# Banded heads of a hybrid decoder layer: turns and value products moved later in the round, weights split sooner, query chunks laid out evenly

## The chip, the cores and the metric

The kernel runs on one core of one Trainium2 chip. The metric is the device time of one execution in microseconds, the median of the runs shown. The profile is one execution taken by the hardware profiler; its times count from the first instruction. TensorE is called PE in its rows, VectorE DVE, ScalarE ACT, GpSimd POOL, and SyncE, which here only sends transfers, SP.

## What is computed

One decoder layer on 2048 tokens of width 1024. The input is RMS-normalised and modulated, projected once, and feeds two kinds of heads side by side: eight heads of causal attention with a cumulative forget gate (called fox below), and eight banded heads, which look back over 128 keys, with rotary positions and one learned sink per head. Both outputs are gated, concatenated, projected, normalised and added to the input. The part that the change touches is the banded one:

```python
def sliding_window_sink_attention(q, k, v, sinks):
    qb = q.reshape(B, nb, Q_BLOCK, SWA_KV_HEADS, SWA_GROUP, d)
    kk, vv = with_prev(k), with_prev(v)
    s = jnp.einsum('bnqhgd,bnshd->bnhgqs', qb, kk, preferred_element_type=jnp.float32) * (d ** -0.5)
    rel = i + Q_BLOCK - j
    band = (rel >= 0) & (rel < WINDOW)
    s = jnp.where(mask[None, :, None, None], s, -jnp.inf)
    p = jax.nn.softmax(jnp.concatenate([s, sink], axis=-1), axis=-1)[..., :-1]
    out = jnp.einsum('bnhgqs,bnshd->bnqhgd', p.astype(vv.dtype), vv)

def reference(x, c, positions, w_ada, b_ada, g_pre, w_in, b_fgate, sinks, w_out, g_post):
    ...
        h = rms_norm(x, g_pre[l]) * (1.0 + scale[:, None, :]) + shift[:, None, :]
        qa, ka, va, fa, za, qb, kb, vb, zb = jnp.split(h @ w_in[l], split_points, axis=-1)
        oa = forgetting_attention(...) * jax.nn.silu(za)
        ob = sliding_window_sink_attention(rope(qb), rope(kb), vb, sinks[l]) * jax.nn.silu(zb)
        y = jnp.concatenate([oa, ob], axis=-1) @ w_out[l]
        x = x + gate[:, None, :] * rms_norm(y, g_post[l])
```

## The kernel before

Every matmul operand is held as two float16 halves, a high one and what is left of it, and each product is made of three matmuls (high by high, high by low, low by high). The order on all engines is written out by hand: what the Python code issues first stands first in its engine's queue, and engines meet through semaphores.

**Stages.** The input is normalised and turned (up to some 130 us, with the keys and values of the banded heads); then comes the banded stage (some 155 to 430 us), in which projections of gates (`zb`), fox values (`va`) and banded queries (`qb`) are the filling between the steps of the banded heads; then the fox stage with its own projections (`qk`, `za`), and last the output projection.

**Units.** A projection of one weight column block (a key such as `zb2`, 128 columns) and one chunk of 512 tokens is cut into eight units of three matmuls of 512 columns (`proj_units`, L335) or twelve of 128 (`value_units`, L351). The list `punits` holds them all; `fill(n)` (L1092) issues the next n. `events` hangs the preparation of a key's weights on unit numbers ahead of its first unit: `w_load` (a transfer of 512 KB by GpSimd's queue), `w_max` (the largest magnitude on VectorE, sent out to memory), `w_back` (read back for all partitions), `w_scale`, `w_high` (ScalarE), `w_low` twice (VectorE), `w_done`. The table in `add` (L944) gives each step its lead in units; `zb0` and `zb1` have leads of their own. The raw weights share two buffers, the halves of `zb` and `va` two more, those of `qb` one.

**Ticks.** `after(n, f)` puts f off by n ticks; `tick()` runs what is due. So a chunk's evacuation is spread behind its last unit: a gate takes a tanh and a product one and two ticks later, a query chunk (`evac_rope`, L725) a copy and a half swap through SP one tick later, then cosine at 2, sine at 7, and the halves at 8 and 9. The swap's buffers `qf` and `qs` are single.

**The banded heads** work in 32 pairs (`Pair`, L859; four pairs of heads by eight pairs of query blocks), one round each. The steps of a pair: `scores` (12 matmuls into the one bank pair `pss`), `maxima` (VectorE: a predicated copy folds the two key blocks into one, then the maximum), `exps` (four exponentials on ScalarE into `sm_`), `turn` (four transposes into `pxb`), `split` one tick later (ScalarE copies the high half to `fold`, VectorE subtracts the low one, GpSimd masks each twice into `ptt`, whose rows the profile calls ptb), `pv` (24 matmuls) and an output step one tick later (VectorE, then a store by GpSimd's queue). A query chunk serves two pairs.

A round (L1128 to L1155) issues 8 or 9 units in four parts with a tick ahead of each. Maxima follow the first tick, exponentials the second, and the end of the round is, on TensorE, `pv` of the pair before, `turn` of this pair and `scores` of the next. The list of units in this stage (L1018 to L1036) alternates query chunks with others by the numbers `lim`; several others remain for the end.

Of the kernel before, what the change touches and what calls it, by code (L numbers as in the profile page):

```python
# [11 lines left out]
F16 = mybir.dt.float16  # L12
# [4 lines left out]
ALU = mybir.AluOpType  # L17
AX = mybir.AxisListType

P = 128  # L20
# [4 lines left out]
CH = 512  # L25
# [18 lines left out]
def hybrid_layer(  # L44
# [17 lines left out]
    V, A, G, PE, SP = nc.vector, nc.scalar, nc.gpsimd, nc.tensor, nc.sync  # L62
# [20 lines left out]
    def sm(n, tag):  # L83
        return small.tile([P, n], F32, tag=tag, name=tag)
# [117 lines left out]
    def after(n, f):  # L202
        late.append([n, f])

    def tick():
        now = [f for n, f in late if n <= 1]
        late[:] = [[n - 1, f] for n, f in late if n > 1]
        for f in now:
            f()
# [15 lines left out]
    def w_max(key):  # L225
        mx = sm(1, "w_mx")
        V.tensor_reduce(mx[:], wq[key][0][:], axis=AX.XY, op=ALU.max, apply_absolute_value=True)
        md = mx_d[len(kaps_seen) % 3]
        kaps_seen.append(key)
        G.dma_start(md[:], mx[:])  # L230
        wq[key].append(md)
# [224 lines left out]
    st = start.enter_context(tc.tile_pool(name="start", bufs=1, reuse_waits="tile"))  # L456
    wad = start.enter_context(tc.tile_pool(name="wad", bufs=8, reuse_waits="tile"))
    with tc.manual_schedule():
# [95 lines left out]
        for _ in range(3):  # L554
            e = math.floor(math.log2(rest))
# [154 lines left out]
    def swa_pool(name, bufs, **kw):  # L710
        return swa.enter_context(tc.tile_pool(name=name, bufs=bufs, reuse_waits="tile", **kw))
# [3 lines left out]
    stp = swa_pool("stp", 2)  # L715
# [143 lines left out]
    class Pair:  # L859
# [40 lines left out]
        def turn(self):  # L900

            px = ps_t.tile([P, 4, P], F32, tag="t", name="pxb")
            for n in range(4):
                PE.transpose(px[:, n, :], self.sm_[:, n, 1:P + 1], ident[:])
            self.ptt = ptp.tile([P, 2, 2, 4, P], F16, tag="pt", name="ptb")
            fold = ptp.tile([P, 2, 4, P], F16, tag="fo", name="fold")

            def split():
                A.activation(fold[:, 0], px[:], AF.Copy)
                V.tensor_tensor(fold[:, 1], px[:], fold[:, 0], op=ALU.subtract)  # L910
                self.rinv = sm(4, "b_ri")
                V.reciprocal(self.rinv[:], self.rs[:])
                for n in range(2):
                    G.affine_select(self.ptt[:, 0, n], fold[:, n], [[0, 4], [-1, P]], ALU.is_ge, 0.0,
                                    base=-1, channel_multiplier=1)
                    G.affine_select(self.ptt[:, 1, n], fold[:, n], [[0, 4], [1, P]], ALU.is_ge, 0.0,
                                    base=0, channel_multiplier=-1)

            after(1, split)

        def pv(self):
            j, i = self.j, self.i
            po = ps_pv.tile([P, 4, 64], F32, tag="pv", name="pob")
            for e, (i_, k0, nk) in enumerate(self.blocks):
                for h in range(2):
                    for b in range(nk):
                        for n, (pp_, vv) in enumerate(((0, 0), (0, 1), (1, 0))):
                            PE.matmul(po[:, 2 * e + h, :], self.ptt[:, b + 2 - nk, pp_, 2 * e + h, :],  # L928
                                      vb[:, k0 + b, self.g, 64 * vv:64 * vv + 64],
                                      start=(b == 0 and n == 0), stop=(b == nk - 1 and n == 2))  # L930

            def out_():
                on = onp.tile([P, 2, P], F32, tag="on", name="on")
                V.tensor_tensor(on[:].rearrange("p e (h d) -> p (e h) d", h=2), po[:],
                                self.rinv[:].unsqueeze(2).broadcast_to([P, 4, 64]), op=ALU.mult)
                o_store(on[:], onp, i // 4, slice((i % 4) * P, (i % 4 + 2) * P), slice((4 + j) * P, (5 + j) * P), G, 1)

            after(1, out_)
# [5 lines left out]
    def add(key, us):  # L944
        if key not in pkeys and key not in ("kb", "vb"):
            at = len(punits) - {"za3": 4}.get(key, 20 if key[:2] == "za" else 0)
            for n, (lead, f) in enumerate(((42, lambda: w_load(key, pieces(key))), (31, lambda: w_max(key)),
                                           (21, lambda: w_back(key)), (12, lambda: w_scale(key)),
                                           (9, lambda: w_high(key)), (7, lambda: w_low(key, 0)),
                                           (5, lambda: w_low(key, 1)), (4, lambda: w_done(key)))):  # L950
                if n >= 4 and key[:2] in ("qk", "za"):
                    lead -= 1
                if n < 4 and key == "qb0":
                    lead += (16, 14, 12, 4)[n]
                if key == "zb1":
                    lead = at - (6, 38, 46, 67, 71, 73, 75, 77)[n]
                if key == "zb0":
                    if n >= 3:
                        events.setdefault((13, 13, 14, 15, 16)[n - 3], []).append(f)
                else:  # L960
                    events.setdefault(max(at - lead, n), []).append(f)
        if key not in pkeys:
            pkeys.append(key)
        punits.extend(us)

    events = {}
    others = []
    for kind, j in (("zb", 0), ("zb", 1), ("va", 0), ("zb", 2), ("zb", 3), ("va", 1), ("va", 2)):
        key = f"{kind}{j}"
# [55 lines left out]
    qbs = [(f"qb{c_ // 4}", qb_units(c_ // 4, c_ % 4)) for c_ in range(2, 16)]  # L1025
    n_o = 7
    for n, (key, us) in enumerate(qbs):
        add(key, us)
        lim = (7, 8, 8)[n] if n < 3 else 5 + 5 * (n + 1) // 4 if n + 1 < len(qbs) else len(others)
        for key2, us2 in others[n_o:lim]:  # L1030
            add(key2, us2)
        n_o = lim
# [56 lines left out]
    windows = [Pair(j, i) for j in range(4) for i in range(0, NB, 2)]  # L1089
    pos = [0]  # L1090

    def fill(n, each=None):  # L1092

        for _ in range(n):
            for f in events.pop(pos[0], []):
                f()
            punits[pos[0]]()
            pos[0] += 1
            if each:
                each()  # L1100
# [9 lines left out]
    with swa_order:  # L1110
        fill(N_PRO - 4, tick2)
        psx.close()
        sws = swa_pool("sws", 1)
        ptp = swa_pool("ptp", 1)
        ps_s = swa_pool("ps_s", 1, space=PSUM)
        ps_t = swa_pool("ps_t", 1, space=PSUM)
        ps_pv = swa_pool("ps_pv", 1, space=PSUM)
        wsp = swa_pool("wsp", 2)
        wss, wst = sm(16, "a_m"), sm(2, "wst")
        wsq = {}  # L1120
        base = N_PRO
        NW = len(windows)
        windows[0].scores()
        windows[0].maxima()
        fill(2, tick2)
        windows[0].exps()
        fill(2, tick2)
        for n, wd in enumerate(windows):  # L1128
            goal = base + (N_SWA - base) * (n + 1) // NW
            todo = goal - pos[0]  # L1130
            part = [todo * (m + 1) // 4 - todo * m // 4 for m in range(4)]
            tick()
            if n:
                wd.maxima()
            fill(part[0])
            tick()
            if n:
                wd.exps()
            fill(part[1])
            tick()  # L1140
            fill(part[2])
            tick()
            fill(part[3])
            if n:
                windows[n - 1].pv()
            wd.turn()
            if n + 1 < NW:
                windows[n + 1].scores()

            if n:  # L1150
                A.activation(wsq[n - 1][:], wsq[n - 1][:], AF.Square, accum_out=wss[:, (n - 1) % 16:(n - 1) % 16 + 1])
            if n == 16:
                V.tensor_reduce(wst[:, 0:1], wss[:], axis=AX.X, op=ALU.add)
            wsq[n] = wsp.tile([P, 2 * P], F32, tag="wsq", name="wsq")
            SP.dma_start(wsq[n][:], w_out0[n // 4 * P:(n // 4 + 1) * P, n % 4 * 2 * P:(n % 4 + 1) * 2 * P])  # L1155
        tick()
        fill(5)
        tick()
        fill(5)
        tick()  # L1160
        fill(6)
        windows[NW - 1].pv()
        tick()
        tick()
        A.activation(wsq[NW - 1][:], wsq[NW - 1][:], AF.Square, accum_out=wss[:, 15:16])
        V.tensor_reduce(wst[:, 1:2], wss[:], axis=AX.X, op=ALU.add)
        wsum = sm(1, "w_mx2")
        V.tensor_reduce(wsum[:], wst[:], axis=AX.X, op=ALU.add)
# [16 lines left out]
    stp = foxl.enter_context(tc.tile_pool(name="stpa", bufs=3, reuse_waits="tile"))  # L1185
# [404 lines left out]
    with tc.manual_schedule():  # L1590
# [34 lines left out]
        for s, stp_ in enumerate(steps):  # L1625
# [11 lines left out]
            a = b = 0  # L1637
# [100 lines left out]
```

## Time and profile before

| | us |
|---|---|
| median of 3 runs | 1173.02 (1172.4 to 1174.38) |
| the profiled execution | 1175.42 |
| its span, first to last instruction | 1173.7 |
| TensorE busy over the span | 1129.2 |
| TensorE busy, 480 to 940 us (fox) | 454.18 of 460 |
| TensorE busy, 1000 to 1174 us (output) | 165.17 of 174 |
| mean granted clock of TensorE | 0.991 of full |

A row of a group gives line, engine, operation and tiles, how often, and times; "idle before" is the time its engine stood, with what ended it. A row of the timeline gives start, duration, engine, line and tiles, and in brackets the idle time just before it with its releaser; neighbours of one kind are merged. In the table by stretches each engine has its busy time and its number of instructions, and PEclk is the share of full clock that TensorE was granted. A busy TensorE may still contain short waits between merged matmuls.

### The profile page before, as it was taken

To read this page: it belongs to the slowest core of one execution; us is meant where nothing else is said; L and a number is where in the kernel's file an instruction comes from. 1 tells how busy PE (TensorE), PEld (TensorE's weight loads), DVE (VectorE), ACT (ScalarE), POOL (GpSimd) and SP (SyncE) were. 2 spreads that over 40 slices of the span, in tenths; PEclk is the share of its full clock that TensorE was granted. 3 is DMA by queue.
4 is the path that set the end of the run, shared out by engine and by line. 5 is a ranking of instruction groups with operands and counts; after the bars stand their busy time and mean duration, and the time that the engine had idled before them with its cause. 6 is when DMAs were issued, how large, how long until landed. Compare 5 with 4: busy or idle time off the path is not lost.

```text
span 1173.7 us, 26784 instructions
## 1 busy us (share of the span) xinstructions
PE 1129.2 (96%) x10637; PEld 671.6 (57%) x10637; DVE 920.0 (78%) x2137; ACT 661.1 (56%) x1150; POOL 196.6 (17%) x332
## 2 busy tenths in 40 slices
PE   6899999999999999999999999999999999999997
PEld 2476545765558976555555565555556555544444
DVE  7777448687776748788888989887897897778885
ACT  2775325455554521476766667676666788543332
POOL 1122124446445521010000100001000000000000
PEclk9899999999999999999999999999999999999999
DMA  9933342424243333423435331222311237677743
GB/s 334 314 101 88 92 70 53 98 53 118 79 73 90 72 69 64 67 61 81 73 71 77 96 60 51 61 53 65 51 34 46 69 86 230 135 216 200 195 144 108
DMA packets 123482, 120.19 MB, mean 102 GB/s; under 512 B 64948, under 2 KB 100828, under 8 KB 123356
## 3 DMA queue, kind: packets, MB, share of 16 engines
q1 hardware_dynamic: 112088, 85.69, 27.0%
q0 software_dynamic: 10832, 32.50, 13.7%
q8 instruction: 83, 1.36, 0.6%
q14 instruction: 43, 0.35, 0.2%
q10 hardware_dynamic: 436, 0.28, 0.1%
HBM read 64.75 MB, written 25.18 MB: 77 GB/s over the span
## 4 chain that ended last, share of the span: by engine, by line
PE 73%; DVE 13%; DMA 6%; ACT 3%; issue 2%; SPq 1%; POOL 1%; ACTq 0%; DVEq 0%
PE bk L344 27%; PE bk L1531 13%; PE bk L362 5%; PE sta L1320 4%; PE sta L1319 4%; PE bk L1270 4%; PE poa L1345 3%; PE poa L1346 3%; PE poa L1343 3%; DMA wa<-in_w_ada_dram 2%; DVE a_m L1273 2%; DVE pha L1333 1%; PE pob L928 1%; PE pss L875 1%; PE bk L781 1%
## 5 line engine op out<-in xcount | busy, mean ns | idle before, releaser
L1326 ACT ACTIVATE p<-sta,lift,scl_qk 128x1024 f32<-128x1024 f32 (+2 forms) x160 | 171.8, 1074 | 130.9 <-PE sta L1320 81.9
L344 PE MATMUL bk<-hT,wh_qk 128*128 128x512 f16 x768 | 194.7, 378 | 0.0
L1333 DVE TENSOR_TENSOR pha<-p,pha 128x1024 f16<-128x1024 f32 (+2 forms) x160 | 169.1, 1057 | 0.2 <-ACT pha L1330 0.2
L1273 DVE TENSOR_REDUCE a_m<-bk 128x1 f32<-128x512 f32 x192 | 130.4, 686 | 48.8 <-PE bk L1270 47.9
L1531 PE MATMUL bk<-wohl,oz 128*128 128x512 f16 x744 | 165.3, 379 | 1.0 <-DVE oz L1480 0.7
L1330 ACT ACTIVATE pha<-p 128x1024 f16<-128x1024 f32 (+2 forms) x160 | 148.1, 926 | 6.0 <-PE poa L1346 1.2
L1531 PEld LDWEIGHTS <-oz 128*128 128x128 f16 x744 | 71.8, 99 | 82.8 <-DVE oz L1480 1.8
L1346 PE MATMUL poa<-vt,pha 128*128 128x65 f16 x1088 | 116.1, 192 | 1.4 <-DVE pha L1333 1.4
L1343 PE MATMUL poa<-vt,pha 128*128 128x65 f16 x1088 | 116.6, 193 | 0.8 <-DVE ona L1352 0.7
L1345 PE MATMUL poa<-vt,pha 128*128 128x64 f16 x1088 | 116.6, 194 | 0.0
L344 PEld LDWEIGHTS <-wh_qk 128*128 128x128 f16 x768 | 72.2, 97 | 74.4 <-issue 1.9
L1270 PE MATMUL bk<-T 66*128 66x512 f16 (+2 forms) x320 | 109.7, 348 | 5.2 <-DVE a_m L1273 1.9
L1319 PE MATMUL sta<-T 128*128 128x512 f16 (+1 forms) x320 | 110.9, 346 | 2.8 <-ACT p L1326 2.7
L1343 PEld LDWEIGHTS <-pha 128*128 128x128 f16 x1088 | 101.5, 96 | 15.5 <-DVE ona L1352 1.9
L1320 PE MATMUL sta<-T 69*128 69x512 f16 (+1 forms) x320 | 109.8, 348 | 0.0
L1345 PEld LDWEIGHTS <-pha 128*128 128x128 f16 x1088 | 100.9, 97 | 11.4
L1346 PEld LDWEIGHTS <-pha 128*128 128x128 f16 x1088 | 100.8, 99 | 1.8 <-DVE pha L1333 1.8
L344 PE MATMUL bk<-hT,wh_za 128*128 128x512 f16 x384 | 99.7, 378 | 0.0
L362 PE MATMUL bk<-wh_va,hT 128*128 128x128 f16 x1536 | 90.6, 219 | 2.5 <-DVE wh_va L267 2.5
L362 PEld LDWEIGHTS <-hT 128*128 128x128 f16 x1536 | 87.3, 98 | 7.3 <-issue 5.1
L344 PE MATMUL bk<-hT,wh_zb 128*128 128x512 f16 x384 | 90.1, 382 | 0.0
L344 PE MATMUL bk<-hT,wh_qb 128*128 128x512 f16 x384 | 87.3, 379 | 0.0
(457 smaller groups left out, 1906.0 us busy)
## 6 DMA issues: line engine op xcount, KB each, us to landing
hT<-in_x_dram SPq DMA_DIRECT2D x20, 512.0 KB
wa<-in_w_ada_dram SPq DMA_DIRECT2D x16, 512.0 KB
z_d<-tz POOLq DMA_DIRECT2D x32, 256.0 KB, 2.9
T<-stq SPq DMA_DIRECT2D x64, 128.0 KB
T<-z_d SPq DMA_DIRECT2D x16, 512.0 KB
out_dram<-hT SPq DMA_DIRECT2D x15, 512.0 KB
xt<-in_x_dram SPq DMA_DIRECT2D x12, 512.0 KB
qs<-qf SPq DMA_DIRECT2D x80, 64.0 KB
```

Source lines behind the costliest of these rows:

```text
L344: PE.matmul(ps, whl[:, a, k, :], hT[ci][:, b, k, :], start=(k == 0 and n == 0), stop=(k == KT - 1 and n == 2))
L362: PE.matmul(ps[:, u * P:(u + 1) * P], hT[ci][:, a, k, u * P:(u + 1) * P], whl[:, b, k, :], start=(k == 0 and n == 0), stop=(k == KT - 1 an ...
L1270: PE.matmul(mx[:, :w], T[0:XM, 0, i * P:(i + 1) * P], T[0:XM, 2, pc * CH:pc * CH + w], start=True, stop=True)
L1273: V.tensor_reduce(m3[:, u, pc:pc + 1], mx[:, :w], axis=AX.X, op=ALU.max)
L1319: PE.matmul(self.st[:, o:o + w], T[:, 3, kb_], T[:, 1, qc], start=True, stop=False)
L1320: PE.matmul(self.st[:, o:o + w], T[0:XR, 2, kb_], T[0:XR, 0, qc], start=False, stop=not diag)
L1326: A.activation(self.p32[:, :self.w], self.st[:, :self.w], AF.Exp, scale=scl[f"qk{self.hd}"][:], bias=lift[:])
L1333: V.tensor_tensor(self.ph[:, 1, :self.w], self.p32[:, :self.w], self.ph[:, 0, :self.w], op=ALU.subtract)
L1343: PE.matmul(po[:, u, :], ph[:, 0, pq], vt[:, b, hd, 0:65], start=(self.first and n == 0 and u == 0), stop=False)
L1345: PE.matmul(po[:, u, 0:64], ph[:, 0, pq], vt[:, b, hd, 65:VW], start=False, stop=False)
L1346: PE.matmul(po[:, u, :], ph[:, 1, pq], vt[:, b, hd, 0:65], start=False, stop=(self.last and n == len(self.blocks) - 1))
L1531: PE.matmul(py, self.hl[:, i, k, :], w_slot(8 * j + k)[:, cc], start=(k == 0 and m_ == 0), stop=(k == KT - 1 and m_ == 2))
```

## The change

Four things. The masked halves of a pair go to two tiles of their own, from one pool for even pairs and from another (the pool `stp`, whose two buffers nothing else uses in this stage) for odd ones, so two pairs can be under way; the exponentials get a second buffer. In the round, `turn` of pair n-1 follows the second part and `pv` of pair n-2 the third, where before `turn` of pair n and `pv` of pair n-1 stood at its end; behind the last round two turns and products are left instead of one product. The leads of `zb` and `va` keys grow by 8 units, that of `va1` by 18 (`zb0` and `zb1` keep theirs, which are set below). And `lim` lets one other chunk follow each query chunk, sometimes two.

```diff
-            self.ptt = ptp.tile([P, 2, 2, 4, P], F16, tag="pt", name="ptb")
+            even = (8 * self.j + self.i // 2) % 2 == 0
+            self.ptt = [ptp.tile([P, 2, 4, P], F16, tag=f"pt{b}", name="ptb") if even else
+                        stp.tile([P, 2, CH], F16, tag="st", name="ptb") for b in range(2)]
+            ptt = [t[:].rearrange("p a (n c) -> p a n c", n=4) if not even else t[:] for t in self.ptt]
+            self.ptt = ptt
             fold = ptp.tile([P, 2, 4, P], F16, tag="fo", name="fold")
...
                 for n in range(2):
-                    G.affine_select(self.ptt[:, 0, n], fold[:, n], [[0, 4], [-1, P]], ALU.is_ge, 0.0,
+                    G.affine_select(ptt[0][:, n], fold[:, n], [[0, 4], [-1, P]], ALU.is_ge, 0.0,
                                     base=-1, channel_multiplier=1)
-                    G.affine_select(self.ptt[:, 1, n], fold[:, n], [[0, 4], [1, P]], ALU.is_ge, 0.0,
+                    G.affine_select(ptt[1][:, n], fold[:, n], [[0, 4], [1, P]], ALU.is_ge, 0.0,
                                     base=0, channel_multiplier=-1)
...
-                            PE.matmul(po[:, 2 * e + h, :], self.ptt[:, b + 2 - nk, pp_, 2 * e + h, :],
+                            PE.matmul(po[:, 2 * e + h, :], self.ptt[b + 2 - nk][:, pp_, 2 * e + h, :],
...
                 if n < 4 and key == "qb0":
                     lead += (16, 14, 12, 4)[n]
+                if key[:2] in ("zb", "va"):
+                    lead += 18 if key == "va1" else 8
                 if key == "zb1":
                     lead = at - (6, 38, 46, 67, 71, 73, 75, 77)[n]
...
-        lim = (7, 8, 8)[n] if n < 3 else 5 + 5 * (n + 1) // 4 if n + 1 < len(qbs) else len(others)
+        lim = 7 + 6 * (n + 1) // 5 if n + 1 < len(qbs) else len(others)
...
-        sws = swa_pool("sws", 1)
+        sws = swa_pool("sws", 2)
...
             fill(part[1])
+            if n:
+                windows[n - 1].turn()
             tick()
             fill(part[2])
+            if n > 1:
+                windows[n - 2].pv()
             tick()
             fill(part[3])
-            if n:
-                windows[n - 1].pv()
-            wd.turn()
             if n + 1 < NW:
                 windows[n + 1].scores()
...
         tick()
         fill(5)
+        windows[NW - 1].turn()
         tick()
         fill(5)
+        windows[NW - 2].pv()
         tick()
         fill(6)
         windows[NW - 1].pv()
```

## The prediction, before the change was run

> **What bounds the kernel now.** I read the page first, then the busy times by stretch for the stage the change touches (about 155 to 430 us), then the waits of TensorE there, then its instructions in order of time.
>
> ```profile
> span 1173.7 us, 26784 instructions
> PE 1129.2 (96%) x10637; PEld 671.6 (57%) x10637; DVE 920.0 (78%) x2137; ACT 661.1 (56%) x1150; POOL 196.6 (17%) x332
> PE 73%; DVE 13%; DMA 6%; ACT 3%; issue 2%; SPq 1%; POOL 1%; ACTq 0%; DVEq 0%
> ```
>
> TensorE is busy 96% of the span and is 73% of the chain that ended last. The change adds and removes no matmul, so it can only take away stretches in which TensorE stands still or runs slowly. How many are there in the banded stage?
>
> ```profile
> core 0: us, PE busy (x) PEld busy (x) DVE busy (x) ACT busy (x) POOL busy (x), PEclk, DMA share, GB/s
> 155.00:210.00 55.00, 50.76 (x486) 30.35 (x484) 37.30 (x93) 24.36 (x76) 18.66 (x31) 0.97 0.40 70
> 210.00:260.00 50.00, 49.55 (x600) 33.86 (x597) 37.77 (x89) 26.51 (x85) 22.83 (x35) 1.00 0.31 72
> 260.00:310.00 50.00, 50.00 (x412) 26.63 (x411) 38.71 (x93) 26.10 (x84) 25.84 (x41) 1.00 0.36 93
> 310.00:360.00 50.00, 48.30 (x497) 29.15 (x496) 34.31 (x77) 27.86 (x93) 26.98 (x43) 1.00 0.43 95
> 360.00:410.00 50.00, 50.00 (x862) 44.91 (x859) 35.44 (x85) 25.97 (x85) 25.39 (x40) 1.00 0.34 68
> ```
>
> TensorE idles 4.2 us in the first of these stretches, 0.5 in the second, 1.7 in the fourth and nothing in the others: 6.4 us, which is 0.5% of the span. VectorE is busy 183.5 of the 255 us (72%), ScalarE 130.8 (51%). So this is a stage with small stalls, not one with a second bound. What the stalls wait for, in the waits of TensorE and of its weight loads between 100 and 430 us (total, times, longest):
>
> ```profile
> PE bk L362 <- DVE wh_va L267: 2.5, 2, 1.6
> PE pob L928 <- POOL ptb L916: 2.5, 3, 1.2
> PE pob L928 <- POOL ptb L914: 0.4, 1, 0.4
> ...
> PEld pxb L904 <- ACT sm__1992 L897: 1.2, 4, 0.3
> PEld pxb L904 <- ACT sm__2714 L897: 0.8, 3, 0.3
> PEld pxb L904 <- ACT sm__3469 L897: 0.6, 2, 0.3
> ...
> PEld pxb L904 <- ACT sm__3158 L897: 0.3, 1, 0.3
> ```
>
> There are three kinds: value products that wait for the masked halves from GpSimd (2.9), value projections that wait for the low half of their weights (2.5), and transposes that wait for exponentials of their own pair (2.9; the weight-load view shows them, the busy times do not, since four stretched transposes look busy). The largest group, in order of time on TensorE:
>
> ```profile
> 172.29 0.23 PE L928 MATMUL pob<-vb,ptb 128*128 128x64 f16 x2 [1.24 <-POOL ptb L916]
> 173.46 0.64 PE L928 MATMUL pob<-vb,ptb 128*128 128x64 f16 x16 [0.94 <-POOL ptb L916]
> 174.25 1.67 PE L904 MATMUL pxb<-ident,sm__1992 128*128 128x128 f32 x4
> ...
> 184.45 0.86 PE L928 MATMUL pob<-vb,ptb 128*128 128x64 f16 x24
> 185.15 0.64 PE L904 MATMUL pxb<-ident,sm__2106 128*128 128x128 f32 x4
> 185.72 0.83 PE L875 MATMUL pss<-kst,stb 64*128 64x256 f16 x12
> ...
> 192.32 0.86 PE L928 MATMUL pob<-vb,ptb 128*128 128x64 f16 x24
> ```
>
> Pair 1 waits 2.2 us for the masks and 1.0 in its transposes (1.67 against the 0.64 of pair 2). A quiet round, from one pair's value products to the next, is 192.32 - 184.45 = 7.9 us. The clock follows the stall:
>
> ```profile
> 172.00:180.00 8.00, 6.29 (x43) 3.05 (x44) 5.46 (x15) 4.38 (x13) 3.81 (x7) 0.79 0.22 59
> ```
>
> A granted clock of 0.79 over 8 us is 0.21 x 8 = 1.7 us of TensorE's work lost. The Trainium skill ("TensorE: Matmul & The Clock Gate", Part 1: The HAM clock gate) puts the halving after a full idle window of some 3.4 us; here pieces of 1.2, 0.9 and 1.0 us within 5 us were enough. [...]
>
> What is behind this group is an earlier event:
>
> ```profile
> 154.12 0.91 POOL L221 DMA_DIRECT2D wr_va<-in_w_in_dram  x1 [0.32 <-issue]
> ...
> 155.33 12.53 DMA qs<-qf
> ...
> 167.88 0.69 DVE L750 TENSOR_TENSOR qs<-qs,sinT 128x512 f32<-128x512 f32 x1 [6.25 <-DMA qs<-qf]
> ```
>
> The half swap of a query chunk, sent just after a weight load of 512 KB, took 12.5 us; VectorE stood 6.25 us in front of it, and the maxima of pair 1, behind it in order, came late.
>
> **The change part by part.** (1) *Turn a half to a whole round later, value products one pair later still.* Nothing is added: 4 transposes, one fold, one subtraction, 4 masks and 24 matmuls per pair, as before. In round n TensorE now transposes pair n-1 after its second part and multiplies pair n-2 after its third. What the moved steps wait for, and how long that has been done:
>
> ```profile
> 202.77 0.60 ACT L909 ACTIVATE fold<-pxb 128x512 f16<-128x512 f32 x1 [0.49 <-PE pxb L904]
> 203.40 0.69 DVE L910 TENSOR_TENSOR fold<-pxb,fold 128x512 f16<-128x512 f32 x1 [0.46 <-ACT fold L909]
> 203.45 0.63 POOL L914 TENSOR_SCALAR_AFFINE_SELECT ptb<-fold 128x512 f16<-128x512 f16 x1 [1.85 <-ACT fold L909]
> 204.09 0.68 DVE L883 COPY_PREDICATED pss<-dmask,pss 128x512 f32<-128x512 int16 x1
> 205.73 0.23 DVE L890 TENSOR_SCALAR b_nb<-b_m,nscl_qb 128x4 f32<-128x4 f32 x1
> 206.08 0.46 ACT L897 ACTIVATE sm__2523<-pss,b_nb,scl_qb 128x129 f32<-128x129 f32 x1 [2.40 <-DVE b_nb L890]
> 207.40 0.46 ACT L897 ACTIVATE sm__2523<-pss,b_nb,scl_qb 128x129 f32<-128x129 f32 x1
> ```
>
> Maxima take 204.09 to 205.96 = 1.9 us, the exponentials 206.08 to 207.86 = 1.8. Before, fold and subtraction (202.77 to 204.09 = 1.3) stood ahead of the maxima, and the transposes of the same pair behind the exponentials, all within one round. Now the exponentials are ready some 3.8 us after the scores, and their transposes come about 11 us after them (a round of 7.9 and two parts of four): 7 us of cover. The masks (4 x 0.63 = 2.5) start some 5 us into a round, and the product that reads them comes 5 us into the next; the cover left is 7.9 - 2.5 = 5.4 us. Both kinds of wait go: -2.9 and -2.9, and with them the slow clock, -1.7. The second probability buffer and the second set of mask tiles are what makes this possible; they cost no instruction. One wait stays: the score bank is single, so the scores of pair n+1 still need the exponentials of pair n. They arrive 7.9 - 0.8 = 7.1 us after the scores of pair n, against 3.8: cover 3.3 us. At the ends, rounds 0 and 1 lose a transposition group and a product each that come back behind the last round: 0.
>
> (2) *Weights sooner.* The third and fourth banded gate keys and three value keys move by 8 units (8 x 0.66 = 5.3 us at 5.93 us for 27 matmuls, below), the second value key by 18. Each moves a 512 KB load, a maximum, two small transfers, a scale, a high half and two low halves, in number unchanged. The load stands in GpSimd's queue (0.91 us to issue) ahead of the masks; its buffer has always been read out by then (the closest, the second value key, loads 9 units after the last reader), so nothing queues behind a wait that was not there. Waits on the halves of value weights: -2.5.
>
> ```profile
> 275.00 5.93 PE bk L344 x27
> ```
>
> (3) *Query chunks spread.* Two query chunks no longer stand side by side, so the single swap buffers are free when the next chunk comes. All but the first of the fourteen now end 8 or 16 units later. The smallest margin to the pair that reads a chunk is 27 units, 3.1 rounds, of which the rotation takes 9 of 4 ticks a round, 2.25: 0.8 round or 6.5 us is left. Cost 0; with the cover gone, the scores would wait, and all of TensorE behind them.
>
> (4) *What comes new.* VectorE works in order, and the subtraction now waits for a fold that stands behind the exponentials on ScalarE. From one pair's maxima to the next this makes a loop: maxima 1.9, exponentials 1.8, what ScalarE has between, fold 0.6, subtraction 0.7, and what VectorE has behind. It must fit 7.9. By bounds: of VectorE's 0.72 x 7.9 = 5.7 us a round, 3.1 are neither maxima nor subtraction; none of them behind the fold gives 5.0, all of them 8.1, with the whole of ScalarE's other work (0.51 x 7.9 - 2.4 = 1.6) between, 9.7. Read off the program's order, 1.9 of the 3.1 and 0.4 of the 1.6 stand there on average: 7.3. It fits, but not in each round. The worst is round 7, where the third gate key is split:
>
> ```profile
> L261 ACT ACTIVATE wh_zb<-wr_zb,w_sw x4: 1143/1148/1152, 60.6 to 295.6; 128x1024 f16<-128x1024 f32 x4
> L267 DVE SCALAR_TENSOR_TENSOR wh_zb<-wr_zb,w_sw,wh_zb x8: 734/746/1189, 61.8 to 298.0; 128x512 f16<-128x512 f32 x8
> L750 DVE TENSOR_TENSOR qs<-qs,sinT x16: 681/690/694, 111.6 to 343.3; 128x512 f32<-128x512 f32 x16
> ```
>
> 5.0 + 1.15 + 2 x 0.75 + 2 x 0.69 (both rotation steps alike) = 9.0, and a value copy, its two lows and an output multiply, some 2 us more: 11. The lag of 3.1 just uses the cover of 3.3. I charge 0.7 here, and 0.8 for what the first swap keeps of its delay (below). Sum: -2.9 - 2.9 - 1.7 - 2.5 + 1.5 = **-8.5 us**. The profiled execution took 1175.42 us for its span of 1173.7 and gives 1166.9; the median of the runs is 2.4 lower, 1173.02, and gives **1164.5**. With none of the 1.5 spent, and with the 1.0 us of idle time that no row above names (6.4 - 2.9 - 2.5), it would be 1162; on the other side stands the loop's 9.7, which is a rival below.
>
> **The rivals.** *The first group stays* because a transfer made it, not the order. The second query key's load now comes 8 units before the point where the value load stood; if the swap again takes 12.5 us, pair 1's exponentials end where they did, and the scores of pair 2 wait in the place of its transposes. Then 2.2 + 1.2 + 1.7 = 5.1 come back, of which 0.8 is charged already: 1169. For it: a load still goes out a few us before that swap. Against: other loads leave swaps of later chunks unharmed (one wait of this kind in 16 chunks).
>
> *The gain is eaten* by lags like that of round 7: rounds 16 to 19 and 26 to 29 are nearly as full. Three places at 3 us, the full lag, take 9 us: 1173. For it: 11 us against 7.9. Against: 7.3 on average, so a lag is gone two rounds on.
>
> *Slower*: the loop through VectorE becomes the bound. It decides from an average loop over 7.9, 0.6 above my count; waits between engines and queueing that I left out could be that much. At 8.4, 30 rounds x 0.5 = 15 us of new waits stand against 10 removed: 1178. The same page of the Trainium skill (Part 1, architectural detail) has ScalarE's and VectorE's queues as strictly first in, first out, which is what makes the loop; the row at 167.88 agrees, with 6.25 us for everything behind one swap. The trace for it: VectorE is at 72%. Against: between 260 and 310 us VectorE is 77% busy (38.71 of 50) and TensorE loses nothing.
>
> **How the numbers follow.** Forecast 0.52, first group stays 0.17, eaten 0.13, slower 0.18. The second lies beyond 0.2% (2.3 us, about what a measurement of this kernel tells from no change), the third within it. Faster 0.69, same 0.13, slower 0.18. The forecast's own range is 1162 to 1168; for 8 in 10 it reaches from 1161 (the 1162 above, less 1 for the spread of the runs, 1172.4 to 1174.38) up through the first two rivals and the milder part of the third, to 1176.
>
> **What would show it.** Right: no wait of TensorE for ptb or wh_va between 150 and 430 us; transposes at 0.64 throughout; clock 1.00 between 172 and 180; the last window's products some 8 us earlier, and later stages of the same length. The first rival: a swap of over 10 us near 155 and scores (pss) behind exponentials. The second and third: weight loads of the score matmuls waiting for exponentials or VectorE in rounds 8, 20 and 29, or in all. Wrong altogether: the stage shortens, and the attention stage behind it grows by as much.

## The result, and the profile after

The changed kernel takes 1169.2 us (median of 13 runs, 1166.98 to 1172.59) against 1174.38 for the kernel before on the same chip (13 runs): a ratio of 0.9952 with a 95% interval of 0.9939 to 0.9964, so 5 to 6 us faster where 8.5 were forecast. (The ratio is worked out from the runs and not from the two medians, so it differs a little from their quotient.) The span of the profiled execution is 4.5 us shorter. Its page:

```profile
span 1169.2 us, 26841 instructions
PE 1124.9 (96%) x10637; PEld 671.1 (57%) x10637; DVE 925.9 (79%) x2137; ACT 661.1 (57%) x1150; POOL 202.9 (17%) x332
```

As many matmuls, 4.3 us less of busy TensorE: some stretched runs are gone. Its idle time over the span is nearly what it was (44.5 us before, 44.3 now). Where the gain lies is shown by the length of the banded stage, from the first matmul of scores (pss) to the last of value products (pob). Both are the first and last starts in the views of these two tiles, of the kernel before and then of the changed one:

```profile
L875 PE MATMUL pss<-kst,stb x384: 216/269/417, 155.4 to 408.7; 64*128 64x256 f16 x180, 64*128 64x128 f16 x12
L928 PE MATMUL pob<-vb,ptb x744: 192/193/203, 172.3 to 427.5; 128*128 128x64 f16 x186
```

```profile
L875 PE MATMUL pss<-kst,stb x384: 216/269/280, 156.7 to 404.6; 64*128 64x256 f16 x180, 64*128 64x128 f16 x12
L932 PE MATMUL pob<-vb,ptb x744: 192/193/193, 177.8 to 424.5; 128*128 128x64 f16 x186
```

The stage went from 427.5 - 155.4 = 272.1 to 424.5 - 156.7 = 267.8 us, that is -4.3. It began 1.3 us later (this start lies between 154.2 and 156.7 in the twelve profiles of this study), and what follows it took 1.5 us less, of which more below. The stage's length leaves both out, and the experiments use it beside the medians. It comes from one execution each, though, so it does not tell kernels apart that differ by a microsecond or two.

The busy times by stretch, in the columns of before:

```profile
155.00:210.00 55.00, 55.00 (x593) 35.81 (x591) 42.97 (x99) 25.77 (x86) 20.02 (x32) 1.00 0.35 73
210.00:260.00 50.00, 46.24 (x487) 29.92 (x484) 36.91 (x87) 25.76 (x83) 24.39 (x36) 0.97 0.33 81
...
310.00:360.00 50.00, 48.75 (x544) 31.85 (x542) 39.40 (x94) 27.62 (x90) 27.51 (x42) 1.00 0.31 84
```

Up to 210 us TensorE no longer stands still at all: the whole first group is gone. But it now loses 3.8 us between 210 and 260, and the waits of TensorE from 100 to 430 us name a kind that was not there before:

```profile
PE pss L875 <- ACT sm__3009 L897: 3.8, 1, 3.8
PE pss L875 <- ACT sm__4478 L897: 1.2, 1, 1.2
PE bk L362 <- issue: 0.8, 1, 0.8
PE bk L1236 <- DVE lk L1256: 0.8, 1, 0.8
```

No wait for masks (ptb) and none for the halves of value weights (wh_va) is left, and no transpose waits for exponentials. In their place scores wait for exponentials, once for 3.8 us (the scores of pair 9, at the end of round 8) and once for 1.2 (at the end of round 20). The large one brings the half clock back, in the table of the 12 us around it:

```profile
226.00:238.00 12.00, 8.24 (x90) 5.96 (x88) 9.87 (x23) 7.63 (x26) 5.58 (x9) 0.86 0.26 68
```

0.14 x 12 = 1.7 us, as much as the stall of before had cost (from 232 to 235 us the granted clock is 0.50). How the 3.8 us come about, on VectorE and ScalarE in order of time (some rows left out):

```profile
215.14 0.68 DVE L883 COPY_PREDICATED pss<-dmask,pss 128x512 f32<-128x512 int16 x1
216.79 0.23 DVE L890 TENSOR_SCALAR b_nb<-b_m,nscl_qb 128x4 f32<-128x4 f32 x1
...
221.03 0.69 DVE L914 TENSOR_TENSOR fold<-pxb,fold 128x512 f16<-128x512 f32 x1 [3.68 <-ACT fold L913]
221.63 0.17 DVE L916 RECIPROCAL b_ri<-b_rs 128x4 f32<-128x4 f32 x1
221.72 1.11 DVE L267 SCALAR_TENSOR_TENSOR wh_zb<-wr_zb,w_sw,wh_zb 128x512 f16<-128x512 f32 x1
222.75 0.74 DVE L371 SCALAR_TENSOR_TENSOR vt<-bk,vt 128x256 f16<-128x256 f32 x2
223.42 0.41 DVE L938 TENSOR_TENSOR on<-pob,b_ri 128x256 f32<-128x256 f32 x1
223.75 0.73 DVE L267 SCALAR_TENSOR_TENSOR wh_zb<-wr_zb,w_sw,wh_zb 128x512 f16<-128x512 f32 x1
...
225.55 0.69 DVE L751 TENSOR_TENSOR qc<-qc,qs 128x512 f32<-128x512 f32 x1
226.29 0.27 DVE L882 MEMSET pss<- 128x256 f32 x1
```

```profile
217.12 0.46 ACT L897 ACTIVATE sm__2875<-pss,b_nb,scl_qb 128x129 f32<-128x129 f32 x1 [2.40 <-DVE b_nb L890]
...
218.87 1.15 ACT L261 ACTIVATE wh_zb<-wr_zb,w_sw 128x1024 f16<-128x1024 f32 x1
219.91 0.60 ACT L367 ACTIVATE vt<-bk 128x512 f16<-128x512 f32 x1
220.39 0.60 ACT L913 ACTIVATE fold<-pxb 128x512 f16<-128x512 f32 x1
```

```profile
219.45 0.67 PE L875 MATMUL pss<-kst,stb 64*128 64x128 f16 x12
...
225.18 1.50 PE L362 MATMUL bk<-wh_va,hT 128*128 128x128 f16 x24
230.44 0.83 PE L875 MATMUL pss<-kst,stb 64*128 64x256 f16 x12 [3.76 <-ACT sm__3009 L897]
```

This is round 7. VectorE ends the maxima at 217.0 and, after one short product, stands 3.7 us in front of the subtraction, because the fold it needs stands on ScalarE behind the exponentials, the high half of a gate key and a value copy. Only then come two low halves, the value lows, the output product and the rotation, all ahead of the next maxima. From maxima to maxima it is 226.29 - 215.14 = 11.15 us against a round of 7.9. Those maxima start 6.2 us after their scores have ended (220.1), and the exponentials of pair 8 are ready only at 230.4.

### The profile page after: what moved, and what is told of

It is laid out like the page before. It is cut to its first block, busy times and chain, and to the rows that moved or that the text cites. A ratio compares the mean times of both kernels' runs of the same rounds, so it can differ in the third digit from the quotient of the medians.

```text
span 1169.2 us, 26841 instructions
## 1 busy us (share of the span) xinstructions
PE 1124.9 (96%) x10637; PEld 671.1 (57%) x10637; DVE 925.9 (79%) x2137; ACT 661.1 (57%) x1150; POOL 202.9 (17%) x332
## 4 chain that ended last, share of the span: by engine, by line
PE 74%; DVE 12%; DMA 5%; ACT 4%; issue 3%; POOL 1%; SPq 0%; DVEq 0%; ACTq 0%; POOLq 0%
PE bk L344 28%; PE bk L1540 13%; PE bk L362 5%; PE sta L1329 4%; PE sta L1328 4%; PE bk L1279 4%; PE poa L1354 3%; PE poa L1355 3%; PE poa L1352 3%; DMA wa<-in_w_ada_dram 2%; DVE a_m L1282 2%; PE pss L875 1%; DVE pha L1342 1%; PE pob L932 1%; DMA T<-stq 1%
## 5 line engine op out<-in xcount | busy, mean ns | idle before, releaser
L362 PE MATMUL bk<-wh_va,hT 128*128 128x128 f16 x1536 | 95.0, 220 | 0.8 <-issue 0.8
L344 PE MATMUL bk<-hT,wh_qb 128*128 128x512 f16 x384 | 90.7, 379 | 0.0
```

The source lines that it names most:

```text
L344: PE.matmul(ps, whl[:, a, k, :], hT[ci][:, b, k, :], start=(k == 0 and n == 0), stop=(k == KT - 1 and n == 2))
L362: PE.matmul(ps[:, u * P:(u + 1) * P], hT[ci][:, a, k, u * P:(u + 1) * P], whl[:, b, k, :], start=(k == 0 and n == 0), stop=(k == KT - 1 an ...
```

## The experiments

All kernels compute the whole layer. The stage is taken from one profile each; for 7, 9 and 10 the profiled execution was the fastest of its runs, so their stages may be short. The ratio is to the kernel before, run beside them on the same chip, with its 95% interval. Experiments 1 to 4, 5 to 8, and 9 and 10 ran on one chip each.

| kernel | median us | ratio | stage us |
|---|---|---|---|
| before | 1174.4 to 1174.8 | 1 | 272.1 |
| changed | 1169.2 | 0.9952 (0.9939 to 0.9964) | 267.8 |
| 1 fold ahead of the exponentials | 1163.7 | 0.9911 (0.9887 to 0.9934) | 263.3 |
| 2 squares a round later | 1166.4 | 0.9931 (0.9909 to 0.9954) | 266.4 |
| 3 third gate key at its old lead | 1163.5 | 0.9906 (0.9881 to 0.9930) | 263.1 |
| 4 new order alone | 1179.0 | 1.0033 (1.0017 to 1.0050) | 278.7 |
| 5 leads and chunks alone | 1175.6 | 0.9999 (0.9981 to 1.0016) | 274.1 |
| 6 new order and chunks, old leads | 1173.0 | 0.9978 (0.9961 to 0.9995) | 272.9 |
| 7 new order alone, fold ahead | 1172.0 | 0.9970 (0.9951 to 0.9989) | 267.6 |
| 8 1 and 3, squares later, shorter lead | 1163.1 | 0.9888 (0.9863 to 0.9912) | 262.2 |
| 9 old order, chunks, leads as in 3 | 1169.8 | 0.9962 (0.9949 to 0.9976) | 265.9 |
| 10 1 and 3 | 1165.2 | 0.9921 (0.9906 to 0.9936) | 263.0 |

**1. The fold ahead of the exponentials**, against the changed kernel:

```diff
             fill(part[0])
+            if n:
+                windows[n - 1].turn()
             tick()
             if n:
                 wd.exps()
             fill(part[1])
-            if n:
-                windows[n - 1].turn()
             tick()
```

> The turn of pair n-1 stands after the first part instead of the second, so its fold stands ahead of the exponentials of pair n on ScalarE. Theory (the fold behind the exponentials makes VectorE's round too long): VectorE's waits for the fold, 39.0 us in the changed kernel, fall below 25; the wait of the scores for exponentials near 226 us, 3.8 us, falls below 1 and the clock there stays at 1.00; 1165 against 1169. Rival (the weights' work itself is too much for those rounds, whatever the order): the wait stays at 2 to 4 us and the time within 1.5 us of the changed kernel.

TensorE's longest waits from 100 to 430 us, then the table around the old stall:

```profile
PE pss L875 <- ACT sm__4494 L897: 1.3, 1, 1.3
PE bk L362 <- issue: 1.0, 1, 1.0
...
PE pss L875 <- ACT sm__3025 L897: 0.2, 1, 0.2
```

```profile
220.00:232.00 12.00, 11.84 (x181) 9.79 (x180) 11.62 (x24) 6.36 (x21) 4.67 (x7) 1.00 0.23 58
```

The 3.8 us became 0.2 and the clock stays full, though VectorE has the same work and is busy 11.62 of these 12 us. The waits of the subtraction, in the changed kernel and then here (from the view of the fold):

```profile
  DVE fold L914: 39.0, 24
```

```profile
  DVE fold L914: 1.2, 3
```

So the order did it, as the theory had it, and more than it had said (below 25 was expected). The stage is 4.5 us shorter than in the changed kernel.

**2. The squares a round later** (one buffer more, `wsq[n - 2]` in place of `wsq[n - 1]`):

```diff
-        wsp = swa_pool("wsp", 2)
+        wsp = swa_pool("wsp", 3)
...
-            if n:
-                A.activation(wsq[n - 1][:], wsq[n - 1][:], AF.Square, accum_out=wss[:, (n - 1) % 16:(n - 1) % 16 + 1])
+            if n > 1:
+                A.activation(wsq[n - 2][:], wsq[n - 2][:], AF.Square, accum_out=wss[:, (n - 2) % 16:(n - 2) % 16 + 1])
...
```

> The squares of the output weights, which ScalarE takes at the end of each round, wait for a transfer sent two rounds before instead of one. In the changed kernel such a wait held ScalarE until 207.8 us and brought a lag of 2.7 us into round 7. Theory (the loop needs the lag to become a stall of 3.8): the wait near 226 us falls to about 1 us, the slow clock behind it goes, 1166. Rival (the loop of round 7 alone, 11 us, makes the stall): the wait stays above 3 us and the time at 1169.

In the waits of TensorE of this kernel the stall is nearly whole:

```profile
PE pss L875 <- ACT sm__3008 L897: 3.3, 1, 3.3
```

The rival was right on the wait, and the clock is still 0.86 over 12 us here. The lag at the start of round 7, from the end of a pair's scores to the start of its maxima, fell only from 2.8 to 2.3 us, so most of it does not come from the transfer. The median is 2.8 us lower than the changed kernel's, which the rival did not expect, but the intervals of the two ratios overlap, and in the profiles 2.5 us of the difference lie before the stage and 1.4 in it.

**3. The third gate key at its old lead:**

```diff
-                    lead += 18 if key == "va1" else 8
+                    lead += {"va1": 18, "zb2": 0}.get(key, 8)
```

> The third gate key alone keeps its old lead, so its high and low halves move out of round 7 into round 8, beside other work. Theory: the wait near 226 us falls below 1.5 us and a smaller one may come a round later; 1166 to 1168. Rival (the squares' transfer holds ScalarE, not the split): the wait stays at about 3.8 us, 1169.

```profile
PE pss L875 <- ACT sm__4478 L897: 1.3, 1, 1.3
...
PE pss L875 <- ACT sm__3186 L897: 0.4, 1, 0.4
PE pss L875 <- ACT sm__3004 L897: 0.2, 1, 0.2
```

These are its waits of scores: the stall is 0.2 us, and 0.4 one pair later. The subtraction still waits 37.0 us in all for its fold. So the fold behind the exponentials alone does no harm here; it takes a round into which a weight split falls as well. In the changed kernel the high half of this key stands on ScalarE between the exponentials and the fold (218.87), here it stands ahead of the exponentials (220.38 against 223.28). Moving this one key by 8 units, which the change did, cost 4.7 us of the stage, about as much as the whole change brought.

**4. The new order alone:** leads and `lim` as before the change.

> The new order and its tiles alone; leads and query chunks as before the change. Theory: no waits of TensorE for masks, the waits for value weights come back (2.5 us), query chunks side by side bring the transfers' delays back, and VectorE's waits for the fold are as in the changed kernel (some 39 us): 1169 to 1172. Rival (the order gives the whole gain and the other two parts cost): 1165 to 1167.

It is slower than the kernel before, by 0.33%. Neither side expected that. Its waits of scores, and two of VectorE's:

```profile
PE pss L875 <- ACT sm__3122 L897: 3.8, 1, 3.8
PE pss L875 <- ACT sm__4254 L897: 2.7, 1, 2.7
PE pss L875 <- ACT sm__1977 L897: 2.6, 1, 2.6
```

```profile
DVE fold L914 <- ACT fold L913: 42.4, 27, 3.0
...
DVE qs L750 <- DMA qs<-qf: 5.6, 2, 5.4
```

The 2.6 us are the first group of before at its old place: the swap came late again (5.4 us in front of VectorE), and with the new order the scores of pair 2 wait instead of the products of pair 0. The other two are crowded rounds (9 and 18). The waits for value weights, which the theory brought back with 2.5 us, came to 0.5.

**5. Leads and chunks alone:** the old order with the new `lim` and leads.

> Leads and query chunks of the change with the old order and one set of tiles. The new order alone took the stage from its first scores to its last products from 272.1 to 278.7 us; the whole change has 267.8. If the parts add up, this gives 267.8 - 6.6 = 261.2, 1163 on the clock. If the new order is what makes the other two worth something (rival), the waits of products for masks and of transposes for exponentials stay and the stage takes 268 to 270: 1169 to 1171.

The parts do not add up, and the rival was still too kind: no gain at all, 0.9999. The waits of its products and transposes:

```profile
PE pob L928 <- POOL ptb L916: 1.5, 3, 0.9
PE pob L928 <- POOL ptb L914: 1.4, 2, 0.9
...
PE pxb L904 <- ACT sm__3046 L897: 1.0, 1, 1.0
```

Of the first group nothing is left: TensorE does not stand still between 165 and 182 us, with the old order.

**6. New order and spread chunks, old leads:**

> The new order with the query chunks spread, but the old leads. Against the order alone (278.7 us for the stage) it shows what the spreading does: I charged nothing for it and gave it nothing. Theory now: chunks side by side put two rotations into one round of VectorE, and spreading them takes away most of the waits of scores for exponentials (2.6, 3.8 and 2.7 us in the order alone): 270 to 272, with a wait for value weights of 1.5 to 3 us left. Rival (the leads do it): 277 or more.

The stage is 272.9 against 278.7 for the order alone: spreading the chunks is worth 5.8 us under the new order. One wait of scores of 2.8 us stays, and the first value units wait 2.6 us in a new place:

```profile
PE pss L875 <- ACT sm__4464 L897: 2.8, 1, 2.8
PE bk L362 <- DVE tz L384: 2.6, 1, 2.6
```

**7. The order alone with the fold ahead of the exponentials:** the diff of 1 on the kernel of 4.

> The order alone, with old leads and chunks, but the turn after the first part, so that the fold stands ahead of the exponentials. Theory (the fold behind the exponentials makes the loop too long): the waits of 3.8 and 2.7 us of the scores in the order alone fall below 1.5 each, VectorE's waits for the fold from 42 to under 10, the stage from 278.7 to 271 to 274. Rival (too much of VectorE's work in one round is enough by itself): both waits stay over 2 us, stage 277 or more.

```profile
PE bk L362 <- issue: 2.5, 1, 2.5
PE pss L875 <- ACT sm__1993 L897: 2.4, 1, 2.4
...
PE pss L875 <- ACT sm__4270 L897: 0.6, 1, 0.6
```

The waits of 3.8 and 2.7 us are down to at most 0.6, and those of VectorE for the fold from 42.4 to 7.1; the one of the late swap (2.4) stays, since its cause is a transfer. (The wait in the first row, near 395 us, has no releaser in the profile.) The stage is 11.1 us shorter than in 4, more than expected, but the runs spread over 1167.8 to 1176.3 us and the profile is of the fastest; the medians differ by 7.0. What differs between the runs was not followed up.

**8. Combined:** 1, 2 and 3 together, and `va1` at 12 units of extra lead instead of 18.

> The change with the turn after the first part, the squares a round later, the third gate key at its old lead and the second value key at 12 units of extra lead instead of 18. The first and third of these alone gave 263.3 and 263.1 us for the stage, with one wait of 1.3 us near 319 us left in each, which the shorter lead of the value key should take away. Theory (each removes its own wait, and both remove the same one near 226 us): stage 261 to 262, 1161 to 1163. Rival (the lead of the value key moves its wait to another round): 263.

1163.1 us, 0.9888: the best kernel here, though 1 and 3 lie within its interval. The expected 261 to 262 us came out at 262.2, but the last wait of scores is still there, at the same pair (318.8 us) and now 1.9 us where 1 and 3 had 1.3. It did not move to another round, as the rival had it, nor go, as the theory had it. The split of the value key did leave this round, but a swap came late in it (VectorE stood 1.5 us in front of it at 312 us):

```profile
PE pss L875 <- ACT sm__4490 L897: 1.9, 1, 1.9
```

**9. The old order with the crowded round cleared:** the diff of 3 on the kernel of 5.

> The old order and one set of tiles, with the new query chunks and leads, but the third gate key at its old lead. It asks what the new order is worth once the crowded round is cleared. With the new order this lead gave 263.1 us for the stage. Theory (the old order ties masks and transposes to the same round, so products wait for masks in other crowded rounds): the waits near 228 us go (about 2.2 and the slow clock 1.7), those near 310 and 418 us stay (2.1 and 1.4): stage 269 to 271, 1170. Rival (with the chunks and leads right the order does not matter): 263 to 265, 1164.

The two measures disagree. The stage, 265.9 us, lies nearer to the rival, the median of 1169.8 agrees with the theory. Against experiment 3 the new order and its tiles are worth 2.8 us by the stages (265.9 and 263.1) and some 6 by the ratios (0.9962 and 0.9906, whose intervals do not meet). Of the waits that were to stay, the one near 418 us is gone and 0.9 us for masks is left (at 303 us). Another, of 1.8 us, has no releaser in the profile:

```profile
PE bk L362 <- issue: 1.8, 1, 1.8
PE pob L928 <- POOL ptb L916: 0.9, 1, 0.9
```

**10. 1 and 3 together:**

> The change with the turn after the first part and the third gate key at its old lead, nothing else. The combined kernel, which also has the squares later and a shorter lead for the second value key, gave 262.2 us for the stage and 1163. Theory (those two give nothing, the one wait of scores left near 319 us comes from the second value and fourth query keys sharing a round): 262 to 263.5, 1163 to 1164. Rival (the squares' transfer matters too): 264 or more.

263.0 us, as the theory had it: no shorter than 1 or 3 alone (263.3 and 263.1). The two remove the same stall, and either is enough. Two waits of scores are left, of 1.3 us (318.96) and 1.2 (310.36). Whether the first comes from the second value key, as the theory had it, stays open: in 8 that key had left the round, and a late swap stood in its place. The median of 1165.2, with runs from 1162.5 to 1167.5, is above the 1163 to 1164 expected; its ratio does not tell it from 1 and 3 alone, since the intervals overlap.

## Why the prediction was right, and where it was off

The direction, the place and the range (1161 to 1176) held; the forecast's own range, 1162 to 1168, did not, and the last products came 3.0 us earlier (427.5 to 424.5), not 8. Of the 4.7 us between the 1164.5 forecast and the 1169.2 measured, 1.4 lie in the base, whose median was 1173.02 in three runs and is 1174.38 in thirteen. By its steps:

**The stalls of before** were read rightly, but for one pair: the products that wait near 172 us are those of pair 0, not 1. Products for masks, transposes for exponentials and value units for their weights are all gone from the views of after. By the start of pair 8's scores the changed kernel stood 8.0 us ahead of the one before (219.45 against 227.49), from 1.3 behind at pair 0; 1.1 of these 9.3 us are only work put off to the end (a group of transposes and one of products).

**The loop through VectorE** was the right mechanism in the right round, with the right length: 11 us was worked out and 11.15 measured. The term that was mis-sized is what it costs: 0.7 was charged, 3.8 and 1.7 of slow clock were paid. "The lag of 3.1 just uses the cover of 3.3" took round 7 as if it began on time. It began 2.8 us late (maxima at 215.14 on scores that ended at 212.4), and the step to it from the maxima before (205.30) took 9.8 us, more than a round, so lags add up: 2.8 + 11.15 - 7.9 is about 6. The cover was too large as well. From the end of pair 8's scores to the start of its maxima the lag is 6.2, 5.7, 2.6 and 2.6 us in the changed kernel and in experiments 2, 3 and 1, and the scores of pair 9 wait 3.8, 3.3, 0.2 and 0.2: each time 2.4 us of the lag are covered, not 3.3. And where the lag ends in a stall, the clock must be counted with it, as the prediction itself had done for the stall of before. Experiment 1 shows that the order makes the loop, experiment 3 that the split makes the round. With 5.5 in the place of 0.7 the sum is -3.7 and the stage shows -4.3, but that they come so close is in part luck, since the terms below were wrong too.

**The first group** was credited to the order, with the swap as a rival. Experiments 4 and 7 bear the rival's mechanism out: with the order alone the swap is late again and the wait (2.6 and 2.4 us) takes the scores' place. In the changed kernel the swap is on time. What moved is the weight load beside it: it was sent at 154.12, behind the start of the chunk's copy at 152.89, and is now sent at 151.57, ahead of that at 154.19. Experiment 5, with the old order, is free of the group too, and so is experiment 6 with the old leads, where the new chunk order moves the load. That the load is what delays the swap was not tested by itself.

**Weights sooner** were credited with the 2.5 us of waits for value weights. But the waits go without the leads as well: with the old ones 0.5 us is left in experiment 4, 0.8 in 6, and none is named in 7. Beside the order and the chunks the leads are worth more than that, for reasons that these rows do not show. The stage is 272.9 us without them (6), 267.8 with them, and 263.1 with all but that of the third gate key (3).

**The chunks** were charged nothing and credited nothing. They are worth 5.8 us of the stage under the new order (6 against 4; the medians differ by 6.0). That term was missing.

**The parts as a sum** was the wrong form. In the stage it is +6.6 us for the order alone, +2.0 for the rest alone, and -4.3 together; by the ratios +0.33%, nothing and -0.48%.

**The gain is eaten** happened in part. Its sign, scores waiting for exponentials, was named for rounds 8, 20 and 29, and it came in two of them, with 3.8 us and the clock in round 8 and 1.2 in round 20.

**Slower** did not happen. The order alone is slower, by the loop through VectorE (experiment 7) and the late swap, but in two crowded rounds and not in all.

**Behind the stage** the profiles differ by 1.5 us that were not forecast. In the kernel before, a weight load of the fox stage stands 2.0 us near 840 us:

```profile
PEld L344 <- issue: 2.0, 1, 2.0
```

In the eleven other profiles no weight load of this line stands for more than 1.0 us behind the banded stage, whichever parts of the change the kernel has, so no one part removed it; it may be chance in that one execution. From the last products to the end of the span the twelve profiles take 743.0 to 746.2 us, so 1.5 us is within their spread.

## What to carry to other kernels

Moving a step later relaxes the engine that used to wait for it, but look at what the step then stands behind on the other engines: a copy behind exponentials held the subtraction, and with it everything behind it on VectorE. Work out the loop from one round's first step to the next for each engine's queue, round by round, and carry the lag from one round to the next; an average that fits says little. And when two parts of a change share a queue, measure each alone before trusting a sum.

## What was not expected of the hardware

One stall of 3.8 us cost 1.7 us more through the clock (0.86 over 12 us), as the shorter pieces near 172 us had; removing it gave the full clock back at the same place (1.00, experiment 1). The length of a stall does not settle it. Single stalls of 2.4 us (7, near 172 us) and 2.8 (6, near 325) brought 0.86 over 12 us too, while one of 2.7 (4, near 317) and one of 2.5 (7, near 395) left the clock at 1.00, and the one of 3.8 in experiment 4 (near 242) brought 0.72.

And one swap of 64 KB pieces beside a weight load held VectorE for 6.25, 5.4 and 5.2 us in the three kernels with the old chunks and leads (before, 4 and 7); in the changed one no rotation waits for its swap. The new chunks and leads do not make that certain: VectorE stood 3.8 us in front of one swap in experiment 5 (near 305 us) and 3.0 in front of one in 8 (near 296).
